# Attention's queries, keys and values in blocks of 512 columns, four heads at a time

## The chip, the cores and the metric

One Trainium2 chip (trn2), one of its cores. The metric is the device time of one execution in microseconds (us); less is better. Several runs of each kernel are made, and their median counts. TensorE multiplies matrices, VectorE and ScalarE work element by element, GpSimd has nearly nothing to do here, and SyncE issues most of the DMA transfers. SBUF is the on-chip memory with 128 partitions. PSUM holds what TensorE writes, in 8 banks; a bank holds 512 float32 columns.

## What is computed

A trunk of four residual layers over 256 tokens of width 2048: an RWKV-7 layer, an attention layer, a pooling layer and a second RWKV-7 layer. The change is in the attention layer:

```python
proj = h @ w_in                                  # 256 x 2048 by 2048 x (9216 + 1024)
qkv = proj[..., :ATT_QKV].reshape(B, S, 3, ATT_GROUPS, ATT_HEADS_PER_GROUP, ATT_HEAD_DIM)
gate = proj[..., ATT_QKV:]
q = _apply_partial_rope(_rms_norm(qkv[:, :, 0], qn_w), cos, sin)   # norm over the 128 of a head
k = _apply_partial_rope(_rms_norm(qkv[:, :, 1], kn_w), cos, sin)   # rotates the first 32 of 128
v = qkv[:, :, 2]
...                                              # softmax attention in 3 dilations, 8 heads each
return (o * silu(gate)) @ w_out
```

There are 3 parts (queries, keys, values) x 3 dilations ("groups") x 8 heads x 128 channels = 9216 columns, then 1024 columns of the gate.

## The kernel before, in words

Products of the projections are made in float32r, a type that TensorE multiplies in one pass. To keep float32's accuracy each operand is split into a high and a low part (`xhi`, `xlo`, `whi`, `wlo`), and three products are added up: high by high, high by low, low by high. `weights` (L186) loads one tile of 128 partitions by 1024 columns (4 k of 256 columns, 512 KB) on SyncE's queue, casts it on ScalarE (L192) and takes the rest on VectorE (L193). Four `raw`, three `whi` and three `wlo` buffers rotate, and two tiles are made ahead (`AHEAD`).

`linear` (L240) goes through blocks of 256 columns; for each of the 16 k it issues 6 matmuls at L289 (2 halves x 3 products). With `tok_major` the hidden state is the stationary operand, which a weight load (LDWEIGHTS) brings into the array, and the weights stream past as 256 moving columns: the result is by token, one PSUM bank for both halves of the tokens. Otherwise the weights are stationary. For each matmul the stationary operand is loaded anew.

After each k `linear` calls `tick` (L196), the planner of the work beside the projections. Generators yield the TensorE time of a step and the delay until the next; `tick(0.64)` moves the plan's time on, and steps that fall due are issued between the matmuls. TensorE takes them in that order. On VectorE and ScalarE a list scheduler may move instructions past each other where their inputs allow it.

`attention` (L944) has 36 token-major blocks: for each quarter (`qr`, two heads) three parts by three groups. `take` (L975) gets a block's PSUM tile. Values are scaled into `vt` on ScalarE (L986). Queries and keys go through `qk_heads` (L1030): square (ScalarE, L1037), sum (VectorE, L1039), the norm's factor (L1041, L1043, L1044), scaling (VectorE, L1046) and the rotation in six small VectorE operations (L1054 to L1056). Some time later `turn` transposes the two heads on TensorE (L998) and copies them to `qT` or `kT` (ScalarE, L1001). When a quarter is complete its two heads join the queue for `attend` (L1059): scores (L1074) in PSUM tiles `scp` of the tag "nt" (two banks), masked into `sc` by VectorE (L1078), a softmax, transposes `ptp` in the tag "sm" (two banks, shared with `tp` of `turn`), their copy to `pt` (L1101), and the product with the values (L1106). A head passes stage A (scores, softmax) and B (the rest), each held by one head at a time. The gate's 4 blocks follow through `take_g` (L1010), then what is left is drained, and `out_proj` multiplies by `w_out`.

The SBUF pools: `wp` (weights), `xp` (split inputs) and `mp` (small tiles, among them `hl`, `mt` and the low-rank tiles of the RWKV layers) live through the kernel; each stage has its own pool on top. The product of the tokens' norm factors, `rs` and `rsc` (L349), is made in `mp`.

Of the kernel before, what the change touches and what calls it, by code (L numbers as in the profile page):

```python
# [15 lines left out]
P = 128  # L16
D = 2048
S = 256
# [7 lines left out]
HLB = 3  # L26
LORA_W = 96
# [65 lines left out]
class Trunk:  # L93
# [69 lines left out]
    # ---------------------------------------------------------------- splits  # L163
    def split(self, src):
        """The two float32r parts of a pair of [128, 256] float32 tiles."""
        nc = self.nc
        hi = self.xp.tile([P, 2, S], F32R, tag="xhi", name="xhi", bufs=9)
        lo = self.xp.tile([P, 2, S], F32R, tag="xlo", name="xlo", bufs=9)
        nc.scalar.copy(hi, src)  # L169
        nc.vector.tensor_tensor(lo, src, hi.bitcast(F32), op=ALU.subtract)  # L170
        return hi, lo

    @staticmethod
    def once(make):
        """xs(k): the parts of tile k, made in pairs when first asked for."""
        made = {}

        def xs(k):
            if k // 2 not in made:
                made[k // 2] = make(k // 2 * 2)  # L180
            hi, lo = made[k // 2]
            return hi[:, k % 2], lo[:, k % 2]

        return xs

    def weights(self, wv, kc, n0):  # L186
# [3 lines left out]
        whi = self.wp.tile([P, 4, NB], F32R, tag="whi", name="whi", bufs=3)  # L190
        wlo = self.wp.tile([P, 4, NB], F32R, tag="wlo", name="wlo", bufs=3)
# [48 lines left out]
    def linear(self, wv, n_lo, n_hi, xs, consume, kt=KT, tok_major=False, rounds=0,  # L240
               wide=False, then=None, blocks=None):
# [6 lines left out]
        blocks = blocks or list(range(n_lo, n_hi, NB))  # L248
# [9 lines left out]
        if then:  # L258
            ch += [(then[0], kc, then[1]) for kc in range(min(self.AHEAD, 4))]
        own = sum(len(c) for c, _, _ in use)  # L260
        pss = None
        for n, (cols, kc, final) in enumerate(use):
# [7 lines left out]
            for k4 in range(4):  # L270
# [8 lines left out]
                for ps, (whi, wlo) in zip(pss, ws):  # L279
                    for m in range(2):  # L280
                        sl = slice(m * P, (m + 1) * P)
                        if tok_major:
                            prod = ((xhi[:, sl], whi[:, k4]), (xhi[:, sl], wlo[:, k4]),
                                    (xlo[:, sl], whi[:, k4]))
                        else:
                            prod = ((whi[:, k4, sl], xhi), (whi[:, k4, sl], xlo),
                                    (wlo[:, k4, sl], xhi))
# [6 lines left out]
            if kc == kt // 4 - 1:  # L294
                for c, ps in zip(cols, pss):
                    if tok_major:
                        consume(n // (kt // 4), ps)
                    else:
                        consume((c - n_lo) // P, ps)
# [12 lines left out]
    def square(self, x, first, last, direct=False):  # L312
        """Adds a pair of tiles of x^T to the sums of squares of the tokens."""
# [35 lines left out]
    def token_scales(self):  # L349
        """The norm's factors of the tokens along a row, and along a column the factors and  # L350
        eps over their squares."""
        nc = self.nc
        self.rs = self.mp.tile([P, S], F32, tag="hl", name="rs", bufs=HLB)
# [7 lines left out]
        c = self.mp.tile([P, 3, 2], F32, tag="rsc", name="rsc", bufs=1)  # L361
# [6 lines left out]
    def norm(self, layer, xt):  # L368
        """h^T of a layer, one zero column ahead of it, from the pairs of tiles of x^T."""
# [17 lines left out]
    def spill(self):  # L387
        """h^T and its token shift's difference to DRAM, for the later projections."""
# [10 lines left out]
    def open_hidden(self):  # L399
        self.hid = ExitStack()  # L400
# [11 lines left out]
    def out_proj(self, wv, xs, kt, li):  # L412
        """x += z @ w_out, then the next layer's norm (or the output)."""
# [35 lines left out]
        if late:  # L449
            w2 = self.i["b_w_in" if layer % 3 == 1 else "c_w_in"][0]  # L450
# [9 lines left out]
    def phase(self, name):  # L460
        return self.tc.tile_pool(name=name, bufs=1)

    # ------------------------------------------------------------------ RWKV
    def mix(self, l, m, k):
        """Two tiles of h + (its token shift - h) mu_m."""
        nc = self.nc
        t = self.mp.tile([P, 2, S], F32, tag="mt", name="mt", bufs=2)
        if self.H is not None:
            self.hmake(k)
        else:  # L470
            h = []
            for q in range(2):
                h.append(self.mp.tile([P, 2, S], F32, tag="hl", name="hl", bufs=HLB))
# [27 lines left out]
    def lora_in(self, l, n, pool, w2, srcs):  # L501
        """The inner activations of the low-rank maps, [rank, 256] each, step by step."""
# [16 lines left out]
        t = self.mp.tile([P, 2, rank], F32, tag="mt", name="lt", bufs=2)  # L519
# [9 lines left out]
        r = self.mp.tile([rank, S], F32, tag="ls" + n, name="ls" + n, bufs=1)  # L529
# [3 lines left out]
    def lora_out(self, out, w2, j, src, rank, key):  # L533
        """max(w0 + src @ w2, ZMIN) - ZMIN of two tiles of 128 channels."""
        nc = self.nc
        wt = self.mp.tile([rank, 2 * P], F32, tag="l2", name="l2", bufs=2)
# [18 lines left out]
    def rwkv(self, l, li):  # L555
# [17 lines left out]
        def take_v(j, ps):  # L573
# [13 lines left out]
            def turn():  # L587
                # centred values by token, columns (head of a tile, tile, channel)
# [59 lines left out]
    def heads(self, l, li, pr, w2, srcs, have):  # L648
        """Four heads (two tiles of 128 channels) of the delta rule, from k^T to the normed output."""
# [7 lines left out]
        # ---- decay, in-context rate  # L657
# [20 lines left out]
        # ---- normalized key, key of the state  # L678
# [36 lines left out]
        # ---- scores  # L715
# [21 lines left out]
        # ---- keys by token  # L737
# [8 lines left out]
        # ---- (1 - N)^-1 of the diagonal blocks of 16, one block in a partition  # L746
# [31 lines left out]
        # ---- blocks of 32, then 64  # L778
# [47 lines left out]
        # ---- centred values by token  # L826
# [9 lines left out]
        # ---- chunks  # L836
# [37 lines left out]
        # ---- norm of a head (its values have no mean), bonus  # L874
# [29 lines left out]
    # ------------------------------------------------------------- attention  # L904
# [39 lines left out]
    def attention(self, li):  # L944
        nc, sp, tc = self.nc, self.sp, self.tc
        T = lambda tag, shape, bufs: sp.tile(shape, F32, tag=tag, name=tag, bufs=bufs)
        H = self.H
        wv = self.i["b_w_in"][0]
# [7 lines left out]
        # rope tables with the norm's weights in them: x1*c, x2*s, x1*s, x2*c  # L956
# [11 lines left out]
        HPB = NB // HEAD  # L968
        cur, left = {}, [0] * (AHEADS // HPB)

        def attend(qr, hd):
            yield from self.attend(hd, qr * HPB + hd, cur[qr], mask, oT)
            left[qr] -= 1

        def take(i, ps):  # L975
            qr, i = divmod(i, 3 * GROUPS)
            part, g = divmod(i, GROUPS)
            if i == 0:
                while qr > 1 and left[qr - 2]:
                    self.tick(0.5)  # L980
                cur[qr] = [T("qT", [P, GROUPS, HPB, S], 2), T("kT", [P, GROUPS, HPB, S], 2),
                           T("vt", [P, 2, GROUPS, HPB * HEAD], 2)]
                left[qr] = 2 * GROUPS + HPB
            if part == 2:
                for tt in range(2):
                    nc.scalar.activation(cur[qr][2][:, tt, g], ps[:, tt], AF.Copy,  # L986
                                         scale=self.rsc[:, 0, tt:tt + 1])
                if g == GROUPS - 1:
                    self.queue += [(attend(qr, hd), lambda: left[qr] <= HPB) for hd in range(HPB)]
                return  # L990
            q5 = self.qk_heads(part, g, ps, tab)

            def turn():
                yield 0.0, 1.0
                tp = self.ps.tile([P, 2, S], F32, tag="sm", name="tp", bufs=2)
                for h in range(2):
                    for t in range(2):
                        nc.tensor.transpose(tp[:, h, t * P:(t + 1) * P], q5[:, t, h],  # L998
                                            self.cst("ident"))
                u = part * GROUPS + g  # L1000
                nc.scalar.activation(cur[qr][part][:, g], tp, AF.Copy, scale=qkw[:, u:u + 1])  # L1001
                left[qr] -= 1
# [3 lines left out]
        blocks = [(part * GROUPS + g) * BRANCH + qr * NB for qr in range(AHEADS // HPB)  # L1006
                  for part in range(3) for g in range(GROUPS)]
        n0 = 3 * GROUPS * BRANCH

        def take_g(j, ps):  # L1010
            t, s = T("gt", [P, 2, S], 2), T("gs", [P, 2, S], 2)
# [5 lines left out]
        def gated(k):  # L1017
# [12 lines left out]
    def qk_heads(self, part, g, ps, tab):  # L1030
        """Norm and rotation of two heads of queries or keys."""
# [3 lines left out]
        p4 = ps.rearrange("p t (h e) -> p (t h) e", h=2)  # L1035
        sq = T("sq4", [P, 4, HEAD], 2)
        nc.scalar.activation(sq, p4, AF.Square, scale=HEAD ** -0.5)  # L1037
# [242 lines left out]
```

## Time and profile before

| | us |
|---|---|
| median of 3 runs | 2302.71 |
| lowest, highest | 2301.54, 2303.0 |
| span of the profiled execution | 2307.1 |
| TensorE busy in it | 2234.1 (97%) |
| VectorE busy | 1586.6 (69%) |
| ScalarE busy | 1301.4 (56%) |
| weight loads (PEld) busy | 2119.4 (92%) |

The span goes from the first to the last instruction of one execution that was recorded; it is 4.4 us above the median of the runs, and no other time of that execution is given. Busy times of TensorE overlap: a matmul starts before the one ahead of it has ended, and the rows' mean durations are longer than the distance between two starts. PE stands for the matmuls, PEld for the weight loads, DVE for VectorE, ACT for ScalarE, SPq for SyncE's queue.

### The profile page before, as it was taken

What the parts mean: (1) busy time and instruction counts of PE and PEld (TensorE: products, weight loads), DVE (VectorE), ACT (ScalarE), POOL (GpSimd) and SP (SyncE); (2) the same over time, 40 slices, a digit from 0 to 9 for tenths busy, and PEclk for the clock granted to TensorE, in tenths of its full rate; (3) what the DMA queues carried; (4) which work ended last, traced back from release to release, by engine and by line L of the source; (5) the groups of instructions that cost most, each with busy time, mean ns of one, the idle gap of its engine ahead of it and who ended that gap; (6) DMA issues with size and microseconds to landing.
All of it is one profiled execution on the core that took longest, in us unless ns stands there. A gap on an engine that the chain in (4) does not pass through costs nothing.

```text
span 2307.1 us, 54751 instructions
## 1 busy us (share of the span) xinstructions
PE 2234.1 (97%) x22762; PEld 2119.4 (92%) x22762; DVE 1586.6 (69%) x2965; ACT 1301.4 (56%) x2074; POOL 4.7 (0%) x12
## 2 busy tenths in 40 slices
PE   7999999999999999999999999999999999999999
PEld 6998888889899999999999999998988888888889
DVE  7678788886556555555557675657678788887654
ACT  6557666665545444444456445546657666666542
POOL 0000000000000000000000000000000000000000
PEclk9999999999999999999999999999999999999999
DMA  7686777756576655454547567776586676665665
GB/s 265 226 259 187 236 212 214 230 155 187 197 249 189 179 151 175 151 177 149 179 150 251 177 183 220 246 220 227 177 282 188 205 230 191 203 194 170 198 212 159
DMA packets 217656, 464.38 MB, mean 201 GB/s; under 512 B 55488, under 2 KB 85824, under 8 KB 217408
## 3 DMA queue, kind: packets, MB, share of 16 engines
q1 hardware_dynamic: 199264, 432.92, 60.7%
q10 hardware_dynamic: 17504, 25.87, 3.2%
q8 instruction: 178, 2.92, 0.5%
q0 software_dynamic: 640, 2.10, 0.2%
q14 instruction: 70, 0.57, 0.1%
HBM read 410.47 MB, written 50.33 MB: 200 GB/s over the span
## 4 chain that ended last, share of the span: by engine, by line
PE 79%; DVE 11%; DMA 6%; ACT 3%; issue 2%; SPq 0%; DVEq 0%; POOL 0%; ACTq 0%; POOLq 0%
PE lin L289 65%; DVE wlo L193 3%; DMA hl<-hd 2%; PE u L515 1%; ACT whi L192 1%; PE yps L870 1%; PE ups L849 1%; DVE xlo L170 1%; PE xps L842 1%; PE q L791 1%; DMA kt<-kd 1%; PE sps L857 1%; PE z L540 1%; PE sc L723 1%; PE op L1106 1%
## 5 line engine op out<-in xcount | busy, mean ns | idle before, releaser
L289 PE MATMUL lin<-xhi,whi 128*128 128x256 f32 x3584 | 1057.5, 296 | 13.4 <-ACT xhi L169 13.2
L289 PE MATMUL lin<-xlo,whi 128*128 128x256 f32 x3584 | 1026.1, 287 | 8.3 <-DVE xlo L170 8.2
L193 DVE TENSOR_TENSOR wlo<-raw,whi 128x1024 fp32r<-128x1024 f32 x600 | 732.3, 1222 | 426.9 <-ACT whi L192 416.0
L289 PE MATMUL lin<-xhi,wlo 128*128 128x256 f32 x3584 | 1023.6, 286 | 0.7 <-DVE wlo L193 0.6
L192 ACT CAST whi<-raw 128x1024 fp32r<-128x1024 f32 x600 | 626.8, 1046 | 543.7 <-PE lin L289 500.1
L289 PEld LDWEIGHTS lin<-xhi,whi 128*128 128x128 f32 x3584 | 691.0, 193 | 36.9 <-ACT xhi L169 16.2
L289 PEld LDWEIGHTS lin<-xlo,whi 128*128 128x128 f32 x3584 | 692.5, 193 | 20.0 <-DVE xlo L170 11.5
L289 PEld LDWEIGHTS lin<-xhi,wlo 128*128 128x128 f32 x3584 | 691.9, 193 | 5.0 <-issue 1.9
L289 PE MATMUL lin<-whi,xhi 128*128 128x256 f32 x1152 | 332.4, 289 | 0.0
L289 PE MATMUL lin<-whi,xlo 128*128 128x256 f32 x1152 | 325.9, 283 | 0.0
L289 PE MATMUL lin<-wlo,xhi 128*128 128x256 f32 x1152 | 325.8, 283 | 0.0
L289 PEld LDWEIGHTS lin<-wlo,xhi 128*128 128x128 f32 x1152 | 221.0, 192 | 0.2
L289 PEld LDWEIGHTS lin<-whi,xhi 128*128 128x128 f32 x1152 | 220.9, 192 | 0.2
L289 PEld LDWEIGHTS lin<-whi,xlo 128*128 128x128 f32 x1152 | 220.8, 192 | 0.0
L478 DVE SCALAR_TENSOR_TENSOR mt<-hl,prm 128x256 f32<-128x256 f32 x152 | 71.2, 476 | 31.9 <-DMA hl<-hd 31.1
L169 ACT CAST xhi<-mt 128x512 fp32r<-128x512 f32 x96 | 58.8, 616 | 44.9 <-DVE mt L478 38.6
L170 DVE TENSOR_TENSOR xlo<-mt,xhi 128x512 fp32r<-128x512 f32 x96 | 65.2, 683 | 5.0 <-ACT xhi L169 4.5
L482 ACT ACTIVATE mt<-H,omm 128x256 f32<-128x256 f32 x120 | 54.2, 501 | 20.8 <-PE u L515 11.2
L484 DVE SCALAR_TENSOR_TENSOR mt<-H,prm,mt 128x256 f32<-128x256 f32 x120 | 52.8, 480 | 15.5 <-ACT mt L482 13.9
L765 DVE TENSOR_TENSOR tmp<-px,Nb 64x15 f32<-64x15 f32 (+7 forms) x240 | 46.7, 194 | 5.8 <-DMA Nb<-ntd 1.2
L768 DVE TENSOR_TENSOR px<-px,tmp 64x15 f32<-64x15 f32 (+7 forms) x240 | 46.8, 195 | 4.5
L723 PE MATMUL sc<-AR,BK 64*128 64x128 f32 x512 | 46.0, 295 | 0.5 <-DVE tmp L765 0.3
(229 smaller groups left out, 2231.6 us busy)
## 6 DMA issues: line engine op xcount, KB each, us to landing
raw<-in_a_w_in_dram SPq DMA_DIRECT2D x256, 512.0 KB, 4.3
raw<-in_b_w_in_dram SPq DMA_DIRECT2D x160, 512.0 KB, 3.5
hl<-hd SPq DMA_DIRECT2D x152, 256.0 KB, 4.5
raw<-in_a_w_out_dram SPq DMA_DIRECT2D x64, 512.0 KB, 4.2
raw<-in_c_w_in_dram SPq DMA_DIRECT2D x64, 512.0 KB, 3.6
raw<-in_c_w_out_dram SPq DMA_DIRECT2D x32, 512.0 KB, 4.2
raw<-in_b_w_out_dram SPq DMA_DIRECT2D x16, 512.0 KB, 4.7
zl<-zd SPq DMA_DIRECT2D x24, 256.0 KB, 4.2
```

The lines of the kernel that those rows point to most:

```text
L169: nc.scalar.copy(hi, src)
L170: nc.vector.tensor_tensor(lo, src, hi.bitcast(F32), op=ALU.subtract)
L192: nc.scalar.copy(whi, raw)
L193: nc.vector.tensor_tensor(wlo, raw, whi.bitcast(F32), op=ALU.subtract)
L289: nc.tensor.matmul(ps[:, m], a, b, start=(k == 0 and m == 0 and q == 0), stop=(k == kt - 1 and q == 2), skip_group_check=True)
L478: nc.vector.scalar_tensor_tensor(t[:, q], h[q][:, 1], mu, h[q][:, 0], op0=ALU.mult, op1=ALU.add)
L482: nc.scalar.activation(t[:, q], self.H[:, k + q, 1:], AF.Copy, scale=self.omm[:, o:o + 1])
L484: nc.vector.scalar_tensor_tensor(t[:, q], self.H[:, k + q, 0:S], mu, t[:, q], op0=ALU.mult, op1=ALU.add)
L515: nc.tensor.matmul(u[:, tt], x[:, q, tt * P:(tt + 1) * P], wt[:, k + q], start=(k + q + tt == 0), stop=(k + q == KT - 1), skip_group_check ...
L723: nc.tensor.matmul(scs[hh][:, c], BK[rows, q, c], AR[rows, hh, q, c], start=True, stop=True)
L765: nc.vector.tensor_tensor(t, px[:, 0:i + 1, 0, i:i + 1].broadcast_to([64, i + 1, w]), Nb[:, i:i + 1, i + 1:].broadcast_to([64, i + 1, w]), ...
L768: nc.vector.tensor_tensor(dst, dst, t, op=ALU.add)
```

## The change

- The weights of queries, keys and values (`b_qkv`) are laid out apart from the gate's (`b_gate`), in tiles of 2 k by 512 columns: 1024 columns and 512 KB as before.
- A new `linear_tokens` goes through 18 blocks of 512 columns. Each block has two PSUM tiles of one bank, one for each half of the tokens, from the tags "lin" and "nt" (two buffers each, so four banks). A matmul streams 512 columns. `tick(0.65)` comes after 6 matmuls.
- `qk_heads` norms and rotates four heads at once. `turn` transposes two pairs of heads in two steps.
- Queries, keys and values of two heads each stand in tiles `qkv` of one tag with 28 buffers, in place of `qT`, `kT` and `vt`; a pair's nine are given back when both its heads are done, and `room` waits if none is left. The heads of a half (four) join the queue together.
- Scores `scp` use the tag "sm".
- `gt` and `gs` of the gate come from the tag "io" of `mp`. `hl`, `mt` and the low-rank tiles get a pool `rw` that is open for an RWKV layer alone; `rs` and `rsc` a pool `tok` on the other side of SBUF.
- Comments and docstrings are dropped.

```diff
+QNB = 512
+QHEADS = QNB // 128
+QBUFS = 28
...
-        raw = self.wp.tile([P, 4, NB], F32, tag="raw", name="raw", bufs=4)
-        nc.sync.dma_start(raw, wv[n0 // NB, kc])
+        k, nb = wv.shape[-2:]
+        raw = self.wp.tile([P, k, nb], F32, tag="raw", name="raw", bufs=4)
+        nc.sync.dma_start(raw, wv[n0 // nb, kc])
...
+    def linear_tokens(self, wv, blocks, xs, consume, then):
+        nc = self.nc
+        kper, nb = wv.shape[-2:]
+        ch = [(wv, kc, c) for c in blocks for kc in range(KT // kper)]
...
+        for n in range(len(blocks)):
+            pss = [self.ps.tile([P, nb], F32, tag=tag, name="lin", bufs=2) for tag in ("lin", "nt")]
+            for kc in range(KT // kper):
+                while len(got) < min(len(ch), done + 1 + self.AHEAD):
+                    got.append(self.weights(*ch[len(got)]))
+                whi, wlo = got[done]
+                done += 1
+                for tt, ps in enumerate(pss):
+                    sl = slice(tt * P, (tt + 1) * P)
+                    for kk in range(kper):
+                        k = kc * kper + kk
+                        xhi, xlo = xs(k)
+                        for q, (a, b) in enumerate(((xhi, whi), (xhi, wlo), (xlo, whi))):
+                            nc.tensor.matmul(ps, a[:, sl], b[:, kk], start=(k == 0 and q == 0),
+                                             stop=(k == KT - 1 and q == 2))
+                        self.tick(0.65)
+            consume(n, pss)
...
-        self.rs = self.mp.tile([P, S], F32, tag="hl", name="rs", bufs=HLB)
+        self.rs = self.tp.tile([P, S], F32, tag="rs", name="rs", bufs=1)
...
+        def room():
+            while live[0] + 2 > QBUFS:
+                self.tick(0.5)
+            live[0] += 2
+            return [T("qkv", [P, 2, S], QBUFS) for _ in range(2)]
...
+                for n, (hp, t) in enumerate(zip(hps, tiles)):
+                    tp = self.ps.tile([P, 2, S], F32, tag="sm", name="tp", bufs=2)
+                    for h in range(2):
+                        for tt in range(2):
+                            nc.tensor.transpose(tp[:, h, tt * P:(tt + 1) * P],
+                                                qs[:, tt, 2 * n + h], self.cst("ident"))
+                    nc.scalar.activation(t, tp, AF.Copy, scale=qkw[:, u:u + 1])
+                    todo[hp] -= 1
+                    yield 0.44, 0.5
...
-        sq = T("sq4", [P, 4, HEAD], 2)
-        nc.scalar.activation(sq, p4, AF.Square, scale=HEAD ** -0.5)
+        for tt in range(2):
+            sq = T("sq4", [P, QHEADS, HEAD], 2)
+            nc.scalar.activation(sq, p4[tt], AF.Square, scale=HEAD ** -0.5)
+            nc.vector.tensor_reduce(ss[:, tt], sq, axis=mybir.AxisListType.X, op=ALU.add)
...
-                sp_ = self.ps.tile([P, 512], F32, tag="nt", name="scp", bufs=2)
+                sp_ = self.ps.tile([P, 512], F32, tag="sm", name="scp", bufs=2)
...
-        self.linear(wv, None, None, hs, take, tok_major=True, blocks=blocks,
-                    then=(wv, n0, hs, False))
-        self.linear(wv, n0, n0 + BRANCH, hs, take_g,
+        wg = self.i["b_gate"][0]
+        self.linear_tokens(self.i["b_qkv"][0], blocks, hs, take, (wg, 0, hs, False))
+        self.linear(wg, 0, BRANCH, hs, take_g,
```

## Rows read from the trace of the kernel before

**Rows 1.** The page: the span, then the token-major matmuls (count; busy us, mean ns).

```profile
span 2307.1 us, 54751 instructions
...
L289 PE MATMUL lin<-whi,xhi 128*128 128x256 f32 x1152 | 332.4, 289 | 0.0
L289 PE MATMUL lin<-whi,xlo 128*128 128x256 f32 x1152 | 325.9, 283 | 0.0
```

**Rows 2.** Busy time by stretch: projection, gate, output projection; granted clock, DMA.

```profile
core 0: us, PE busy (x) PEld busy (x) DVE busy (x) ACT busy (x) POOL busy (x), PEclk, DMA share, GB/s
708.00:1172.00 464.00, 464.00 (x3860) 462.58 (x3860) 265.28 (x466) 222.20 (x325) 0.00 (x0) 1.00 0.55 168
...
1172.00:1222.00 50.00, 50.00 (x420) 49.79 (x419) 31.70 (x41) 29.29 (x44) 0.00 (x0) 1.00 0.49 148
1222.00:1272.00 50.00, 49.92 (x411) 49.51 (x411) 38.27 (x52) 31.30 (x48) 0.00 (x0) 1.00 0.82 265
```

**Rows 3.** The chain in order of time: start us, us, engine, what, how many.

```profile
986.25 11.52 PE lin L289 x96
...
1022.11 28.07 PE lin L289 x234
...
1051.56 0.86 PE scp L1074 x4
```

**Rows 4.** Timeline inside a block: start us, us, engine, line, instruction.

```profile
1029.86 0.28 PE L289 MATMUL lin<-whi,xhi 128*128 128x256 f32 x1
1029.87 0.19 PEld L289 LDWEIGHTS lin<-wlo,xhi 128*128 128x128 f32 x1
1029.98 0.28 PE L289 MATMUL lin<-wlo,xhi 128*128 128x256 f32 x1
```

**Rows 5.** RWKV layer: the chain's 96-column and 512-column products, and one weight load.

```profile
62.06 0.86 PE u L515 x8
...
281.69 0.86 PE gps L882 x2
...
282.38 0.19 PEld L884 LDWEIGHTS bps<-kp,c 128*128 128x128 f32 x1 [0.24 <-issue]
```

**Rows 6.** VectorE's timeline at the end of a block of keys.

```profile
1131.21 0.69 DVE L1039 TENSOR_REDUCE ss<-sq 128x4 f32<-128x512 f32 x1 [1.20 <-ACT sq L1037]
1131.93 0.16 DVE L1041 TENSOR_TENSOR ss<-ss,rsc 128x4 f32<-128x4 f32 x1
1132.14 1.23 DVE L193 TENSOR_TENSOR wlo<-raw,whi 128x1024 fp32r<-128x1024 f32 x1
1133.28 0.68 DVE L1046 TENSOR_TENSOR qs<-lin,ss 128x512 f32<-128x512 f32 x1
...
1134.82 1.22 DVE L193 TENSOR_TENSOR wlo<-raw,whi 128x1024 fp32r<-128x1024 f32 x1
```

**Rows 7.** ScalarE's timeline at the same block's end.

```profile
1130.58 0.60 ACT L1037 ACTIVATE sq<-lin 128x512 f32<-128x512 f32 x1 [1.83 <-PE lin L289]
1131.07 1.04 ACT L192 CAST whi<-raw 128x1024 fp32r<-128x1024 f32 x1
```

**Rows 8.** VectorE's groups by shape, 708 to 1222 us: count; busy us, mean ns.

```profile
L1046 DVE TENSOR_TENSOR qs<-lin,ss 128x512 f32<-128x512 f32 x24 | 16.4, 683 | 0.0
L1054 DVE TENSOR_TENSOR rp<-qs,tab 128x64 f32<-128x64 f32 x96 | 15.2, 220 | 0.8
...
L1078 DVE SCALAR_TENSOR_TENSOR sc<-scp,mask 128x512 f32<-128x512 f32 x8 | 5.5, 686 | 1.0 <-PE scp L1074 1.0
```

**Rows 9.** Who waited for whom, 708 to 1222 us: us in total, times, longest.

```profile
ACT pt L1101 <- PE ptp L1100: 23.7, 19, 2.2
...
DVE sc L1078 <- PE scp L1074: 12.8, 16, 2.0
```

**Rows 10.** The weight tiles `raw`, 708 to 1180 us.

```profile
DMA to landing us min/median/max: 3.3/3.5/5.2
```

More of the change, by code (lines that the diff above doesn't have):

```diff
@@ L238, in part, with linear @@
                     then=then)
-    def linear(self, wv, n_lo, n_hi, xs, consume, kt=KT, tok_major=False, rounds=0,
-               wide=False, then=None, blocks=None):
+    def linear(self, wv, n_lo, n_hi, xs, consume, kt=KT, rounds=0, wide=False, then=None):
         nc = self.nc
-        blocks = blocks or list(range(n_lo, n_hi, NB))
+        blocks = list(range(n_lo, n_hi, NB))
         ch, use = [], []
@@ L258, in linear @@
         if then:
-            ch += [(then[0], kc, then[1]) for kc in range(min(self.AHEAD, 4))]
+            ch += [(then[0], kc, then[1]) for kc in range(self.AHEAD)]
         own = sum(len(c) for c, _, _ in use)
@@ L281, in linear @@
                         sl = slice(m * P, (m + 1) * P)
[L282 to L287, printed above, removed]
+                        prod = ((whi[:, k4, sl], xhi), (whi[:, k4, sl], xlo),
+                                (wlo[:, k4, sl], xhi))
                         for q, (a, b) in enumerate(prod):
@@ L295, in linear @@
                 for c, ps in zip(cols, pss):
[L296 to L299, printed above, removed]
+                    consume((c - n_lo) // P, ps)
+        self.pre = got[own:]
+    def linear_tokens(self, wv, blocks, xs, consume, then):
+        nc = self.nc
+        kper, nb = wv.shape[-2:]
+        ch = [(wv, kc, c) for c in blocks for kc in range(KT // kper)]
+        own = len(ch)
+        ch += [(then[0], kc, then[1]) for kc in range(self.AHEAD)]
+        got, self.pre = self.pre, []
+        done = 0
+        for n in range(len(blocks)):
[15 more added lines that the diff above has]
+            consume(n, pss)
         self.pre = got[own:]
@@ L449, in out_proj @@
         if late:
-            w2 = self.i["b_w_in" if layer % 3 == 1 else "c_w_in"][0]
+            w2 = self.i["b_qkv" if layer % 3 == 1 else "c_w_in"][0]
             then = (w2, 0, whole, True)
@@ L518, in lora_in @@
             yield 0.7, 0.4
-        t = self.mp.tile([P, 2, rank], F32, tag="mt", name="lt", bufs=2)
+        t = self.rp.tile([P, 2, rank], F32, tag="mt", name="lt", bufs=2)
         if n == "w":
@@ L535, in lora_out @@
         nc = self.nc
-        wt = self.mp.tile([rank, 2 * P], F32, tag="l2", name="l2", bufs=2)
+        wt = self.rp.tile([rank, 2 * P], F32, tag="l2", name="l2", bufs=2)
         nc.scalar.dma_start(wt, w2[:, j * P:(j + 2) * P])
@@ L967, in attention @@
         gate = self.kp.tile([P, AHEADS, S], F32, name="gate")
[L968 to L975, printed above, removed]
+        cur = [[[None] * GROUPS for _ in range(3)] for _ in range(AHEADS // 2)]
+        todo = [2 * GROUPS] * (AHEADS // 2)
+        live = [0]
+        def room():
[3 more added lines that the diff above has]
+            return [T("qkv", [P, 2, S], QBUFS) for _ in range(2)]
@@ L976, in take, with attend @@
+        heads = [2] * (AHEADS // 2)
+        def attend(hp, hd):
+            yield from self.attend(hd, hp * 2 + hd, cur[hp], mask, oT)
+            heads[hp] -= 1
+            if not heads[hp]:
+                live[0] -= 3 * GROUPS
+        def take(i, pss):
             qr, i = divmod(i, 3 * GROUPS)
             part, g = divmod(i, GROUPS)
[L978 to L983, printed above, removed]
+            hps = range(qr * QHEADS // 2, (qr + 1) * QHEADS // 2)
+            tiles = room()
+            for hp, t in zip(hps, tiles):
+                cur[hp][part][g] = t
@@ L984, in take @@
             if part == 2:
                 for tt in range(2):
-                    nc.scalar.activation(cur[qr][2][:, tt, g], ps[:, tt], AF.Copy,
-                                         scale=self.rsc[:, 0, tt:tt + 1])
+                    for n, t in enumerate(tiles):
+                        nc.scalar.activation(t[:, tt], pss[tt][:, n * S:(n + 1) * S], AF.Copy,
+                                             scale=self.rsc[:, 0, tt:tt + 1])
                 if g == GROUPS - 1:
-                    self.queue += [(attend(qr, hd), lambda: left[qr] <= HPB) for hd in range(HPB)]
+                    self.queue += [(attend(hp, hd), lambda hp=hp: todo[hp] == 0)
+                                   for hp in hps for hd in range(2)]
@@ L990, in take @@
                 return
-            q5 = self.qk_heads(part, g, ps, tab)
+            qs = self.qk_heads(part, g, pss, tab)
             def turn():
                 yield 0.0, 1.0
[L995 to L999, printed above, removed]
-                u = part * GROUPS + g
-                nc.scalar.activation(cur[qr][part][:, g], tp, AF.Copy, scale=qkw[:, u:u + 1])
-                left[qr] -= 1
+                u = part * GROUPS + g
+                for n, (hp, t) in enumerate(zip(hps, tiles)):
[7 more added lines that the diff above has]
+                    yield 0.44, 0.5
@@ L1004, in take @@
             self.active.append([turn(), "T", None, self.now + 5.0])
-        blocks = [(part * GROUPS + g) * BRANCH + qr * NB for qr in range(AHEADS // HPB)
+        blocks = [(part * GROUPS + g) * BRANCH + qr * QNB for qr in range(BRANCH // QNB)
                   for part in range(3) for g in range(GROUPS)]
-        n0 = 3 * GROUPS * BRANCH
         def take_g(j, ps):
-            t, s = T("gt", [P, 2, S], 2), T("gs", [P, 2, S], 2)
+            t, s = (self.mp.tile([P, 2, S], F32, tag="io", name=n, bufs=4) for n in ("gt", "gs"))
@@ L1028, in attention, with qk_heads @@
         return zs
[L1030 removed]
+    def qk_heads(self, part, g, pss, tab):
         nc, sp = self.nc, self.sp
@@ L1209, in run @@
                         zs = self.stored(li)
+                self.tok.close()
             if li + 1 < len(self.layers) and self.layers[li + 1] % 3 == 0:
                 self.open_hidden()
+            elif li + 1 < len(self.layers):
+                self.tok = ExitStack()
+                self.tp = self.tok.enter_context(self.phase("tok", side="right"))
             with self.phase(f"o{li}") as self.sp:
```

63 lines of the change are left out of this document (33 added, 30 removed).

## The prediction

> **What bounds the kernel now.** I read the page first, for the span and the costliest groups, then the busy time in stretches, to see which engine is full while queries, keys and values are projected. The profiled execution spans 2307.1 us [rows 1]; the three runs have a median of 2302.7, so the profile stands 4.4 us (0.2%) above them. I work out a difference from the profile and take it off the median. About 0.2%, some 4.6 us, is also what a measurement of this kernel can tell from no change.
>
> The stretch from 708 to 1172 us is the token-major projection, and from 1172 to 1222 the gate's. TensorE is busy for all of both, at a granted clock of 1.00, its upper level of 2.4 GHz; VectorE has work in 57% of the first, ScalarE in 48%, and the DMA engines are 55% busy at 168 GB/s [rows 2]. So TensorE's own stream sets the time there, and a change counts as far as it shortens that stream or tears holes in it.
>
> How fast the stream runs is not in the mean duration of a matmul (283 ns, [rows 1]), since matmuls overlap. The chain of waits, in order of time, gives the rhythm: 96 matmuls of 256 columns in 11.52 us, 234 in 28.07 us, so 120.0 ns from start to start [rows 3]. At 2.4 GHz 256 columns are 106.7 ns; 13.3 ns are something else. The timeline says what it may be: a matmul starts at 1029.86, the weight load for the next at 1029.87, the next matmul at 1029.98 [rows 4]. The load starts just after its predecessor's matmul has started, and the next matmul starts some 110 ns later. Each matmul here waits for its own weight load, which takes about as long as the 256 columns before it.
>
> **The change, part by part.**
>
> *Half as many matmuls, twice as wide.* There are 3 x 1152 = 3456 matmuls of 256 columns now [rows 1]; 18 blocks x 16 k x 2 token halves x 3 products = 1728 of 512 columns come instead. Now: 3456 x 119.96 ns = 414.6 us. For a 512-column matmul of this type the trace has no row. Bounds by the nearest rows: at best the columns alone, 213.3 ns (the float32 product gps takes 0.86 us for two passes of 512 columns, about 428 ns each, just two cycles for a column, and the weight load beside it shows 0.24 us of idle time, [rows 5]); at worst twice today's, 240 ns, if the excess grows with the columns. Between them: 226.6 ns, if 13.3 ns are paid once for each matmul. The nearest row in time, not in type, is the float32 score product: four passes of 256 columns at two cycles each, so also 213.3 ns of streaming with a reload for each, take 0.86 us, 215 ns [rows 3]. Where the stream is as short as the load it shows: the low-rank product u, 96 columns and so 80 ns of streaming, still takes 0.86 us for 8, 107.5 ns each [rows 5]. Both say that a load of some 107 ns sets the rhythm until the stream is longer, and is hidden then. I take 215 ns: 1728 x 0.215 = 371.5 us, **43.1 us saved**, and keep 23 us (226.6 ns) and about zero as the other ends.
>
> A rule speaks against this. The Trainium skill (TensorE: Matmul & The Clock Gate, section Back-to-back issue gap) gives the isolated gap of a warm matmul as its columns over 2.4 GHz and 2.5 ns. By it 256 columns would take 109.2 ns and 512 columns 215.8, and halving the count would spare 2.5 ns a time, 4.4 us in all. The trace disagrees at 256 columns by 10.8 ns, and that difference is the forecast gain; no row here shows which holds at 512.
>
> *Weights.* A tile is still 1024 columns by 128 partitions, 512 KB; as many are loaded, cast on ScalarE and split on VectorE (1.05 and 1.22 us). One now feeds 12 matmuls, 2.58 us, where it fed 24 in 2.88. The DMA need rises from some 168 to at most 203 GB/s (512 KB in 2.58 us); the stretch after the gate moves 265 [rows 2], and a tile lands in 3.5 us with four buffers [rows 10]. VectorE's 1.22 and ScalarE's 1.05 us still fit in 2.58. Cost taken: zero.
>
> *Norm and rotation of four heads at once.* The 512-element operations stay as many for a head; the six small ones double their width. By 683 ns for 512 elements and 220 for 64 [rows 8], 1.03 ns an element, one of 128 takes 285 ns, so VectorE is spared about a microsecond for four heads; off the path. What matters is the end of a block, where this work comes in one piece. Now, after the block's last matmul, ScalarE squares (1130.58) and casts the third weight tile (1131.07) [rows 7]; VectorE reduces, adds, splits that tile while it waits for the two small ScalarE steps, scales, rotates and splits the next at 1134.82 [rows 6]. After the change the second half's square ends 0.6 us after the last matmul, the reduce at 1.3, the add at 1.5, the ScalarE steps at 2.0, the two scalings at 3.4, six small ones at 5.1. If the split still slips into that wait, it is done at 2.9; it is wanted by the second matmul of the third tile, 2 x 2.58 + 0.2 = 5.4. If it comes behind the rotation, it ends at 6.3, 0.9 us late, in 12 blocks: 11 us. I take zero, since the wait and the order of priorities stay, and keep 11 us for the range. Waiting behind that split would be the matmuls of the next block.
>
> *Scores move from two PSUM banks of their own to the two that transposes use.* A group of scores now has to wait until an earlier score or transpose has been copied out. Today the copies start as soon as TensorE is done: ScalarE and VectorE sat idle before 19 of 24 copies of transposed weights and 16 of 24 masked scores [rows 9]. A copy takes 0.69 us [rows 8] and may stand behind a split of 1.22, so 1.9 us at most, while between two uses lie at least six matmuls, 1.29 us beside the wide ones and 0.72 beside the gate. So 0.6 or 1.2 us late at worst, for 12 score groups each: 22 us above, zero below. I take 2 us, since most copies found their engine free.
>
> *Due times.* A step of the side work is offered after six matmuls, as before, but these now last 1.29 us and count as 0.65, so in real time the heads are spread twice as far. Four heads are left for the gate's 64 steps where two were. Counted through the delays in the code, the fourth ends at the 55th step; none is left for the drain. Their 5 us each move, they do not grow. The turning steps wait longer, but their tile is wanted 20 us later only. The room for 28 tiles is not short: eighteen of the first half and ten of the second fill it at the fifth block of the second half, and the first nine come back in its second. Zero, and 2 us either way where the last gate passes to the output projection.
>
> *Pools.* Shift and rank tiles get a pool that closes with each RWKV layer, the token factors one on the right; same number of buffers, same queues. No DMA is added or moved past another. Zero, hidden by the projections that run on while the first tiles of the new pool are filled; 2 us either way.
>
> Sum: 43.1 - 2 = **41 us less**: 2302.7 - 41 = 2261.7, about 2266 in a profile.
>
> **Rivals.**
> 1. *A fixed 13.3 ns for each reload.* For it: 120.0 is exactly 32 cycles over 256, and no row of this type is longer. Against it: rows of float32 lose it when they stream longer. It gives 23 us, less 2: 2282.
> 2. *The time goes with the columns,* for instance because moving data of this type arrives at 256 columns in 120 ns and no faster; only what float32 shows is spared, 2 x 215 - 428 = 2 ns a time, 4 us with nothing given back: 2299. For it: every row of this type has that rate. Against it: the weight load that starts at once and ends as the next matmul starts [rows 4]. (The Trainium skill's gap rule named above gives this time too, by another reason.)
> 3. *Slower: the shared PSUM banks become the wait.* TensorE works in order, so one score or transpose that finds no bank free holds all projections behind it. 72 such tiles (24 scores, 24 copies of weights, 24 turned pairs) pass through two banks. Break-even is 43 / 72 = 0.6 us each; at the 1.2 us worked out above it is 86 us: 2302.7 - 43 + 86 = 2346. Against it: the idle engines of [rows 9].
> 4. *The late split* at every block end takes back 11 us: 2273.
>
> **How the numbers follow.** Load hidden, little given back: 0.64, near 2262, itself 2257 to 2267. With the late split: 0.08, 2273. Fixed 13.3 ns: 0.15, 2282. By columns: 0.08, 2299. Shared banks: 0.05, 2346. The likeliest gives 2262. The range takes the first three: 2256 (all of the columns' bound, 213.3 ns, and nothing given back) to 2284; 0.13 is left out. Faster by over 0.2%: 0.64 + 0.08 + 0.15 + 0.02 = 0.89; within it, the rest of the columns' case, 0.06; slower 0.05.
>
> **What would show it.** In the chain of waits, 48 wide matmuls in a row in 10.3 us (215 ns) confirm the main step, 10.9 us the fixed cost, 11.5 us the columns. The stretch from the first query block to the end of the gate should shrink from about 513 to 472 us with TensorE still full. Waits of matmuls of lin on wlo at block ends show the late split; waits of score products or transposes on ScalarE or VectorE show the banks. Weight loads with idle time before them would show that they are hidden. I am wrong if 512 columns take over 235 ns, or if other stretches move by over 4 us.

## The result, and the profile after

The changed kernel is faster, by half of what was forecast.

| | before | after |
|---|---|---|
| median, us (4 runs each) | 2302.86 | 2282.16 |
| lowest, highest | 2301.54, 2305.27 | 2278.24, 2284.08 |
| ratio, 95% interval | | 0.9895 (0.9874 to 0.9917) |
| span of the profiled execution | 2307.1 | 2282.3 |

That is 20.7 us less. 2262 was forecast, with a range of 2256 to 2284; the time lies where the first rival put it, at 2282. The span of a profile leaves out a little under 2 us of the execution's time: the profiled one after took 2284.08 us.

The page gives the new matmuls, which answer to [rows 1]; columns are the count, then busy us, mean ns, idle time before.

```profile
L321 PE MATMUL lin<-whi,xhi 128*128 128x512 f32 x576 | 229.5, 399 | 0.0
...
L321 PE MATMUL lin<-wlo,xhi 128*128 128x512 f32 x576 | 224.4, 390 | 0.0
L321 PEld LDWEIGHTS lin<-whi,xlo 128*128 128x128 f32 x576 | 108.1, 188 | 22.8
```

There are three groups of 576, so 1728 matmuls as counted. Their weight loads now show idle time ahead of them (22.8 us in this group, 0.0 to 0.2 in the groups of before): the loads are hidden, as forecast. The chain of waits, in order of time, answers to [rows 3].

```profile
1055.63 0.44 PE tp L1037 x4
...
1057.20 21.12 PE lin L321 x93
1078.32 0.44 PE tp L1037 x4
...
1249.86 0.86 PE ss L354 x4
```

93 matmuls in 21.12 us are 227.1 ns from start to start, where 240 would be twice the old ones, 226.6 their streaming and 13.3 ns, and 215 was forecast. 48 of them are 10.9 us, which the prediction had named as the sign of the fixed cost. The timeline says the same, and what the load does meanwhile (as in [rows 4]).

```profile
1000.35 0.39 PE L321 MATMUL lin<-whi,xlo 128*128 128x512 f32 x1
1000.35 0.19 PEld L321 LDWEIGHTS lin<-whi,xhi 128*128 128x128 f32 x1
...
1000.58 0.39 PE L321 MATMUL lin<-whi,xhi 128*128 128x512 f32 x1
```

The load for the next matmul starts with the matmul ahead of it, as before, and its row ends at 1000.54; the next matmul starts at 1000.58. The stretch is as full as it was (busy time by stretch, as in [rows 2]: span of the stretch, PE, PEld, DVE, ACT, POOL, granted clock, DMA share, GB/s).

```profile
700.00:1160.00 460.00, 460.00 (x2278) 388.58 (x2277) 269.87 (x396) 233.53 (x319) 0.00 (x0) 1.00 0.54 179
1160.00:1210.00 50.00, 50.00 (x418) 49.58 (x417) 32.83 (x48) 29.77 (x49) 0.00 (x0) 1.00 0.40 130
```

From the first matmul of the queries (708.62 before, 711.99 after) to the sum of squares after the attention's output projection (1267.81 and 1249.86) the stage took 559.2 us and takes 537.9: 21.3 us, the whole of the result. A second profile of the changed kernel, from a run below, has the stage at 537.9 us again. The stage begins 3.4 us later in the first of them and the rest of the kernel is 6.9 us shorter than in the profile of before; in the second it is 3.1 us and 8.4. That is more than the 4 us in other stretches that the prediction had set as a sign of being wrong. There is one profile of the kernel before, and its span stood 4.4 us above the median, so whether the change moves these parts stays open. By the medians they come to nothing together: 20.7 us in all, 21.3 in the stage.

VectorE at the end of a block answers to [rows 6].

```profile
1049.50 0.69 DVE L1078 TENSOR_REDUCE ss<-sq 128x4 f32<-128x512 f32 x1 [0.44 <-ACT sq L1077]
1050.22 0.17 DVE L1079 TENSOR_TENSOR ss<-ss,rsc 128x8 f32<-128x8 f32 x1
1050.44 1.22 DVE L197 TENSOR_TENSOR wlo<-raw,whi 128x1024 fp32r<-128x1024 f32 x1
1051.58 1.28 DVE L1085 TENSOR_TENSOR qs<-lin,ss 128x512 f32<-128x512 f32 x2
1052.78 1.21 DVE L197 TENSOR_TENSOR wlo<-raw,whi 128x1024 fp32r<-128x1024 f32 x1
1053.91 0.89 DVE L1092 TENSOR_TENSOR rp<-qs,tab 128x128 f32<-128x128 f32 x4
```

The split of the third weight tile slips into the wait for ScalarE's two small steps, as forecast, and the fourth even between scaling and rotation, which was not. In the view of waits no matmul, transpose or score of TensorE waits for anything between 700 and 1210 us, so neither the late split nor the shared banks hold TensorE up.

### The profile page after: what moved, and what is told of

Same layout as the page of the kernel before. It is cut to its first block, busy times and chain, and to the rows that moved or that the text cites. A ratio compares the mean times of both kernels' runs of the same rounds, so it can differ in the third digit from the quotient of the medians.

```text
span 2282.3 us, 51163 instructions
## 1 busy us (share of the span) xinstructions
PE 2210.9 (97%) x21034; PEld 2025.7 (89%) x21034; DVE 1578.4 (69%) x2881; ACT 1299.8 (57%) x2050; POOL 4.7 (0%) x12
## 4 chain that ended last, share of the span: by engine, by line
PE 73%; DVE 13%; DMA 8%; ACT 3%; issue 2%; SPq 1%; DVEq 0%; POOL 0%; ACTq 0%; POOLq 0%
PE lin L287 44%; PE lin L321 17%; DMA hl<-hd 3%; DVE wlo L197 3%; PE u L542 1%; DVE xlo L173 1%; ACT whi L196 1%; DMA zl<-zd 1%; DVE mt L505 1%; PE z L567 1%; PE q L818 1%; PE yps L897 1%; DMA kt<-kd 1%; PE xps L869 1%; DVE AR L759 1%
## 5 line engine op out<-in xcount | busy, mean ns | idle before, releaser
L197 DVE TENSOR_TENSOR wlo<-raw,whi 128x1024 fp32r<-128x1024 f32 x600 | 732.4, 1222 | 441.1 <-ACT whi L196 429.7
L321 PE MATMUL lin<-whi,xhi 128*128 128x512 f32 x576 | 229.5, 399 | 0.0
L321 PE MATMUL lin<-whi,xlo 128*128 128x512 f32 x576 | 224.6, 390 | 0.0
L321 PE MATMUL lin<-wlo,xhi 128*128 128x512 f32 x576 | 224.4, 390 | 0.0
L321 PEld LDWEIGHTS lin<-whi,xlo 128*128 128x128 f32 x576 | 108.1, 188 | 22.8
L321 PEld LDWEIGHTS lin<-wlo,xhi 128*128 128x128 f32 x576 | 108.3, 188 | 20.9
L321 PEld LDWEIGHTS lin<-whi,xhi 128*128 128x128 f32 x576 | 108.3, 188 | 20.7
L759 DVE TENSOR_TENSOR AR<-sc,c 64x512 f32<-64x512 f32 x64 | 44.4, 694 | 1.4
```

The lines of the kernel that those rows point to most:

```text
L197: nc.vector.tensor_tensor(wlo, raw, whi.bitcast(F32), op=ALU.subtract)
L321: nc.tensor.matmul(ps, a[:, sl], b[:, kk], start=(k == 0 and q == 0), stop=(k == KT - 1 and q == 2))
L759: nc.vector.tensor_tensor(AR[half[1 - hh], hh, q].rearrange("p c a t -> p c (a t)"), sc[64:128].rearrange("p c a t -> p c (a t)"), mk[64:1 ...
```

## The experiments

What was open: why a 512-column matmul of float32r takes 227 ns and not 215, though its load is hidden; whether the width is the whole of the gain; whether the same cost can be spared elsewhere.

### Bursts of matmuls alone

Edit: the trunk is left out; for each case 48 matmuls on resident data.

```diff
+            for k in range(REP):
+                o = ps[k % 2 if alt else 0]
...
+                nc.tensor.matmul(o[:, :c], w[n][:, k % 2 if two else 0], m[n][:, :c],
+                                 start=bool(first or over), stop=bool(last or over))
```

> This kernel leaves out the whole trunk: it runs bursts of 48 matmuls on resident data and writes a few columns out. Bursts: float32r (r), bfloat16 (b) and float32 (f) at 512, 384, 256 and 128 moving columns with two stationary tiles in turn; the same stationary tile again and again (same); every matmul starting its sum anew (over); two PSUM banks in turn (alt). Theory 1, a fixed cost for each float32r matmul whatever its width: start to start r512 227 ns, r384 174, r256 120, and the line through them has 13 to 14 ns at zero columns; b512 near 215. Theory 2, a cost of each new stationary tile, whatever the type: b512 and b256 show the same 13 ns (227 and 120), b512same and r512same lose it if the load falls away. Theory 3, adding onto the same PSUM bank: r512over or r512alt fall to 215. Theory 4, that the load sets the pace at 256 and something else at 512: r384 lies off the line of the other two, at 174 or below it, and r128 stays near 110 to 120 as r256 does.

The chain shows the last six cases apart; the others share a name here and were run again below. Each kernel of bursts ran once; where the two repeat a case they agree (5.75 us for float32r at 256 columns, 10.38 for bfloat16 at 512).

```profile
178.03 10.93 PE pr512same L1340 x48
188.96 10.38 PE pb512same L1340 x48
199.34 10.90 PE pr512over L1340 x48
210.24 10.88 PE pr512alt L1340 x48
221.12 5.75 PE pr256alt L1340 x48
226.87 5.27 PE pb256same L1340 x48
```

Over 48: float32r takes 227.7, 227.1 and 226.7 ns at 512 columns, whether the stationary tile stays, each matmul starts its own sum, or two banks take turns. So adding onto the same bank (theory 3) is out. Bfloat16 takes 216.3 and 109.8 ns. It too loads the stationary tile for every matmul, the same one again and again as well (288 loads for six bursts of 48):

```profile
L1340 PEld LDWEIGHTS <-bw 128*128 128x128 bf16 x288 | 26.0, 98 | 15.5 <-issue 0.3
```

So a reload as such, whatever the type, costs no 13 ns, and theory 2 is out. The cost goes with float32r. But the load here is the shorter one, 98 ns in its rows where float32r's has 188, so that the length of the load is left as a cause.

The second kernel of bursts gives each width a name, and narrows the stationary tile to 64 and 32 columns.

```diff
+            cases += [(f"_{n}_full_load_half", n, 512, 1, 0, 64),
+                      (f"_{n}_full_load_quarter", n, 512, 1, 0, 32),
+                      (f"_{n}_half_load_half", n, 256, 1, 0, 64)]
...
+                nc.tensor.matmul(ps[:cols, :c], w[n][:, k % 2 if two else 0, :cols], m[n][:, :c],
+                                 start=k == 0, stop=k == REP - 1)
```

> Leaves out the whole trunk, as the first kernel of bursts. Bursts of 48 matmuls by type (r float32r, b bfloat16, f float32) and by moving columns (full 512, three 384, half 256, quarter 128), each with its own name, then with a stationary tile of 64 or 32 columns in place of 128 (load_half, load_quarter). If float32r has a fixed cost for each matmul, which its weight load has no part in: r full 227 ns, three 173, half 120, and full_load_half and full_load_quarter stay at 227, half_load_half at 120; b full 216 and half 110. If the cost is the part of the weight load that can't be hidden, it shrinks with the load: r full_load_half about 220, full_load_quarter about 217, half_load_half about 113. r quarter shows the load's own floor: about 110 for 128 columns.

```profile
17.76 10.88 PE p_r_full L1340 x48
28.64 8.34 PE p_r_three L1340 x48
36.98 5.75 PE p_r_half L1340 x48
42.73 5.31 PE p_r_quarter L1340 x48
48.04 10.38 PE p_b_full L1340 x48
...
66.22 5.24 PE p_b_half L1340 x48
...
74.14 41.26 PE p_f_full L1340 x96
...
146.35 20.72 PE p_f_half L1340 x96
...
177.79 11.04 PE p_r_full_load_half L1340 x48
188.83 11.12 PE p_r_full_load_quarter L1340 x48
199.95 5.45 PE p_r_half_load_half L1340 x48
205.40 10.48 PE p_b_full_load_half L1340 x48
```

| ns from start to start | 512 | 384 | 256 | 128 | 512, load of 64 | 512, load of 32 | 256, load of 64 |
|---|---|---|---|---|---|---|---|
| float32r | 226.7 | 173.8 | 119.8 | 110.6 | 230.0 | 231.7 | 113.5 |
| columns / 2.4 GHz | 213.3 | 160.0 | 106.7 | 53.3 | 213.3 | 213.3 | 106.7 |

Float32r's excess is 13.3, 13.8 and 13.1 ns at 512, 384 and 256 columns: nearly the same at all three widths. At 512 it does not shrink with the load; it grows by 3 to 5 ns (bfloat16's, 10.48 / 48 = 218.3, by 2). At 256 columns half of the load takes away 6.3 ns, so there the load has a part in the pace. At 128 columns 110.6 ns are far above 53.3 and 13; the load is the likely floor there, though no run takes it away at that width. Bfloat16's excess is 3.0 ns at 512 (10.38 / 48 = 216.3) and 2.5 at 256 (109.2). Float32, at two cycles a column in each of its two passes, takes 41.26 / 96 = 429.8 and 20.72 / 96 = 215.8 ns, an excess of 3.1 and 2.5. The forecast took that small excess for float32r, and it is not float32r's. The Trainium skill (TensorE: Matmul & The Clock Gate, section Back-to-back issue gap) gives the isolated gap of a warm matmul as its columns over 2.4 GHz and 2.5 ns; the bursts of bfloat16 agree within 0.5 ns, those of float32r lie 11 ns above it at 256 columns and more.

Float32 also answers the question of the load's length. Its load rows last as long as float32r's:

```profile
L1340 PEld LDWEIGHTS p_f_half<-fm,fw 128*128 128x128 f32 x96 | 18.2, 190 | 2.7
L1340 PEld LDWEIGHTS p_r_full<-rm,rw 128*128 128x128 f32 x48 | 9.0, 188 | 1.9
```

Both kinds of matmul stream for 213.3 ns beside such a load, float32 in 256 columns and float32r in 512, and they take 215.8 and 226.7 ns. So the length of the load alone isn't what costs the 13 ns there.

Nor is it a time that each float32r matmul pays at any clock. In the trace of the kernel before, TensorE waits 5.8 us before 22.66 us, and the granted clock falls to its lower level, 1.2 GHz (first the stretch as in [rows 2], then two starts):

```profile
24.00:28.00 4.00, 4.00 (x19) 4.00 (x20) 4.00 (x10) 3.06 (x7) 0.00 (x0) 0.50 1.02 397
...
24.18 0.41 PE L289 MATMUL lin<-xhi,wlo 128*128 128x256 f32 x1
...
28.02 0.41 PE L289 MATMUL lin<-xhi,whi 128*128 128x256 f32 x1
```

Eighteen float32r matmuls of 256 columns in 3.84 us are 213.3 ns each, which is 256 columns at 1.2 GHz and no excess, though a load row lasts 0.33 us there. The same 213.3 ns of streaming take 226.7 at the upper level.

### The changed kernel with narrow matmuls

```diff
-                            nc.tensor.matmul(ps, a[:, sl], b[:, kk], start=(k == 0 and q == 0),
-                                             stop=(k == KT - 1 and q == 2))
+                            for h in range(2):
+                                cs = slice(h * NB, (h + 1) * NB)
+                                nc.tensor.matmul(ps[:, cs], a[:, sl], b[:, kk, cs],
...
```

> The changed kernel with each 512-column matmul of the token-major projection issued as two of 256 columns into the halves of the same bank; blocks, tiles, pools, banks and heads stay as changed. If the width of the matmul is the whole of the gain: 3456 x 120.0 = 414.7 us in place of 1728 x 227.2 = 392.6, so 22 us more, 2304 us, no difference from before. If the gain lies in the blocks of four heads, the pools or the banks: it stays at 2282.

Measured: 2310.69 us (12 runs) beside 2307.31 of the kernel before in the same session (17 runs), ratio 1.0011 (0.9994 to 1.0028). The chain has the old pace.

```profile
1000.20 22.31 PE lin L323 x186
```

119.9 ns each. In this trace the stage (first matmul of the queries at 709.86, sum of squares at 1269.13) takes 559.3 us, where the kernel before has 559.2. The width is the whole of the gain. Blocks of four heads, 28 tiles, pools, scores in the shared banks and due times together change nothing that can be measured: by the interval, less than 0.3% in either direction.

### Two matmuls for three elsewhere

If each float32r matmul costs 13 ns beyond its columns, the other projections could spare one of three: they multiply the same high weights by the high and by the low input, 256 columns each. A first form, in which both halves of the wide matmul are added onto the same 256 columns of PSUM in all 3648 pairs (2235 us was expected of it), gave no time. The second gives them a bank of their own.

```diff
+                        nc.tensor.matmul(ps, whi[:, k4, sl], x2, start=(k == 0), stop=False,
+                                         skip_group_check=True)
+                        nc.tensor.matmul(ps[:, 1], wlo[:, k4, sl], x2[:, 0], start=False,
+                                         stop=(k == kt - 1), skip_group_check=True)
...
+                if fold:
+                    t = self.sp.tile([P, 2, S], F32, tag="fs", name="fs", bufs=2)
+                    for m, ps in enumerate(pss):
+                        nc.scalar.copy(t[:, m], ps[:, 1])
+                    for m, ps in enumerate(pss):
+                        nc.vector.tensor_tensor(t[:, m], t[:, m], ps[:, 0], op=ALU.add)
```

> The changed kernel, and in the output projections of 16 k, the pooling layer's two projections and the attention's gate (1408 pairs of a k and 128 output columns) two matmuls in place of three: the high weights by high and low input side by side, 512 moving columns into a PSUM bank of their own, then the low weights by the high input, 256 columns, onto one half of it; ScalarE copies one half out and VectorE adds the other at the end of a block. If the fixed cost of 13 to 14 ns for each float32r matmul holds for weights as the stationary operand too: 120.0 + 227.2 = 347.2 ns in place of 360.0, 12.8 x 1408 = 18 us less, given back 1 to 2 us at each of five ends of a stage where the longer way out of PSUM shows: 2266 to 2272 where the changed kernel has 2282 (in the same session, 0.7% less than it). If the cost belongs to the token-major form alone: nothing gained, 2282 to 2292.

> The changed kernel as it is, beside the one before and the side-by-side one on the same chip. All theories: about 21 us under the kernel before, 0.991 of it; the side-by-side kernel is read against this.

Beside 2302.43 us of the kernel before (11 runs), the side-by-side kernel took 2283.83 (6 runs; 0.9911, 0.989 to 0.9932) and the changed kernel 2281.18 (6 runs; 0.9901, 0.9883 to 0.9919), as before. The changed kernel repeated its result; the side-by-side one gained nothing on it. The timeline of the first output projection shows why it is not the matmuls.

```profile
660.00 0.28 PE L288 MATMUL lin<-xhl,wlo 128*128 128x256 f32 x1
660.12 0.40 PE L286 MATMUL lin<-xhl,whi 128*128 128x512 f32 x1
660.35 0.28 PE L288 MATMUL lin<-xhl,wlo 128*128 128x256 f32 x1
...
662.94 0.40 PE L286 MATMUL lin<-xhl,whi 128*128 128x512 f32 x1
```

From 660.12 to 662.94 there are eight pairs, 352.5 ns each, where three matmuls took 360: the cost is spared with weights as the stationary operand too, though less than the 12.8 ns expected. In the last output projection a pair took 347. At 7 to 13 ns for 1408 pairs that is 10 to 18 us gained on the way. The same profile shows what gave it back (waits of TensorE: us in total, times, longest; then the chain's end, as above):

```profile
PE lin L286 <- DVE xhl L173: 8.2, 2, 6.2
PE ss L371 <- ACT sq L366: 3.2, 1, 3.2
```

```profile
2285.80 0.38 ACT fs L305
2286.20 0.78 DVE fs L307 x2
```

VectorE's low parts are the last that the wide matmul waits for, twice, for 8.2 us, where the changed kernel has no such wait on low parts beyond 1.5 us. The sum of squares waits 3.2 us (0.7 in the changed kernel), and 1.2 us lie at the very end. That is 12 us or so. It was expected that five ends would give back 1 to 2 us each; one alone took 6.2. That one, at the start of the last output projection, was not VectorE's doing:

```profile
2212.84 0.62 ACT L172 CAST xhl<-zl 128x512 fp32r<-128x512 f32 x1 [5.23 <-DMA zl<-zd]
...
2214.24 0.80 PE L286 MATMUL lin<-xhl,whi 128*128 128x512 f32 x1 [6.22 <-DVE xhl L173]
...
2218.88 0.53 PE L286 MATMUL lin<-xhl,whi 128*128 128x512 f32 x1
```

ScalarE's cast had itself waited 5.23 us for the transfer of the input, which was issued at 2208.91, after TensorE's last matmul had started (2207.74). So the input came late; that the wide matmul wants high and low at once can add only VectorE's 0.69 us. Why the transfer was issued so late is not shown. After this wait the granted clock fell to 0.50 (2214 to 2218 us), and a pair took 640 ns, six of them from 2215.04 to 2218.88, where it takes 347 at the upper level. Seven pairs lost some 2 us more (an estimate from these two paces). This profile is also the longest of the kernel's six runs, 2292.66 us. In the profiles of the two variants below, at 2283.06 and 2278.3 us, the waits on low parts (7.4 and 8.9 us) and the 3.2 us are there again.

Two variants of it: the two inputs of one k in successive columns, and then the gate left out.

```diff
-        hi, lo = hl[:, 0], hl[:, 1]
+        hi, lo = hl[:, :, 0], hl[:, :, 1]
...
-                    then=(self.i["b_w_out"][0], 0, zs, False), fold=True)
+                    then=(self.i["b_w_out"][0], 0, zs, False))
```

> The side-by-side kernel with high and low input of one k in 512 successive columns of SBUF, where they were two runs of 256; nothing else. In the side-by-side kernel a pair took 353 ns in the first output projection and 347 in the last. If the two runs cost the 6 ns: 347 ns in both, some 4 to 9 us less than the side-by-side kernel, 2275 to 2280. If not: the same time, 2284, and 353 ns stay.

> The kernel with successive columns, but with the attention's gate in three matmuls a pair as in the changed kernel, so that its last block leaves PSUM by the short way ahead of the output projection. 128 pairs of 1408 lose 7 to 13 ns each, 1 to 2 us; the wait of TensorE between gate and output projection (8 us of the chain in the side-by-side kernel) should go: 2 to 5 us less than with the gate. If that wait is made up elsewhere: 1 to 2 us more.

They took 2282.19 us (0.9895, 0.9875 to 0.9916) and 2279.79 (0.9892, 0.9868 to 0.9917) beside 2307.39 of the kernel before.

```profile
661.55 0.28 PE L288 MATMUL lin<-xhl,wlo 128*128 128x256 f32 x1
...
662.94 0.28 PE L288 MATMUL lin<-xhl,wlo 128*128 128x256 f32 x1
```

With successive columns, four pairs in 1.39 us are 347.5 ns in the first output projection; the pooling layer's, whose input comes from another place, kept 353 (1301.86 to 1302.92, three pairs). Two runs of 256 columns went with 352.5 ns in the first output projection and with 347 in the last, successive columns with 347.5 and, in the pooling layer, 353. So the layout alone doesn't decide those 6 ns; what does is open. Leaving the gate out came 2.4 us lower, within the spread of the runs (2277.82 to 2287.03). The wait of TensorE between gate and output projection that it was to take away is gone, but that was 1.9 us; the 8.9 us of waits on low parts lie in the pooling layer and the last one, and stay. The intervals of all these kernels overlap that of the changed one: no version here beats it by an amount that can be measured.

## Why the prediction was right or wrong

- **TensorE's stream sets the time**: right. It is full before and after, at the same clock, and the 21.3 us come from the pace of its matmuls.
- **Half as many matmuls at 215 ns, 43.1 us saved**: the step that failed is the size of this term. They take 227.2 ns: 1728 x 0.2272 = 392.6 us in place of 414.6, 22.0 us saved. The price was taken from the float32 score product, "the nearest row in time, not in type", and from the idle weight load. The load is hidden now, and the next matmul still doesn't start. At the upper clock the bursts show 13 to 14 ns for each float32r matmul at three widths, and 2.5 to 3 for the two other types.
- **That the load sets the rhythm at 256 columns**: a half truth. 128 columns with a load take 110.6 ns, less than 119.8; a shorter load speeds up the 256-column matmul by 6.3 of the 13 ns. What is left when the load is out of the way was read as nothing. The timeline couldn't show it either: the load was read as ending when the next matmul starts [rows 4], but its row, 0.19 us from 1029.87, ends 0.08 us after that start.
- **Rival 1, the fixed cost**: its size is what happened, 13 to 14 ns a matmul at 512 columns as at 256. It was given 0.15. That it is paid "for each reload" is not shown: bfloat16 reloads without it, half a load doesn't lower it at 512 columns, and at the lower clock it is gone. The argument for it, exactly 32 cycles above the columns and no longer row of the type, stood in the prediction; what spoke against it came from another type.
- **Rival 2, time by columns**: refuted by 227.2 against 240. The Trainium skill's rule on the gap, named above, holds in the bursts of bfloat16 and not in those of float32r. It was set against the forecast, yet its 215.8 ns for 512 columns is nearly the price that the forecast took. (2.5 ns for each of 1728 are 4.3 us, not the 4.4 of the prediction.)
- **Shared banks, 2 us; late split, 0 and 11 us**: both are zero. No wait of TensorE is left in the stage, and the narrow kernel, which keeps both, equals the kernel before.
- **Weights, due times, pools at zero**: right, by the narrow kernel, for all of them together.
- **The range** held because it reached to the fixed cost; the likeliest case's own range, 2257 to 2267, did not. That the time lies inside is owed to the width of the range and not to the mechanism that was forecast.

## What to carry to other kernels

A stream of short matmuls may pay a time for each besides its weight load, and the distance of starts at one width can't tell the two apart: two widths of the same type at the same clock can, and the price of another type can't stand in. Where the load is hidden by a wider moving operand, only what each instruction pays is spared. Saving an instruction in a full stream counts only if the inputs at the ends of a stage arrive as early as the faster stream wants them; in the side-by-side kernel one arrived late, and the clock fell behind that wait.

## What was not expected of the hardware

- A float32r matmul costs 13 to 14 ns beyond its columns at 256, 384 and 512 columns, a bfloat16 one 2.5 to 3.0, though both load their stationary tile each time. Float32 with load rows as long as float32r's has 2.5 to 3.1. What in TensorE takes that time is open; float32r came with its load in every trace, so no run shows its matmul without one.
- At the lower level of the clock the excess is gone: 213.3 ns for 256 columns, and 640 ns for a pair of 512 and 256, which are the columns at 1.2 GHz.
- Narrower stationary tiles made 512-column matmuls slower: 226.7 ns at 128 stationary columns, 230.0 at 64, 231.7 at 32 in float32r; 216.3 and 218.3 at 128 and 64 in bfloat16, in one execution.
- A pair of a 512-column and a 256-column matmul took 352.5 or 347 ns by its place in the kernel, and the layout of the moving operand alone does not say which.
